# Low parts on VectorE beside the scans, diagonal blocks copied by VectorE, and the FFN norm's steps inside the out-projection

## The chip, the core and the metric

The kernel runs on one core of one Trainium2 chip. The metric is the device time of one execution in microseconds; lower is better. Before the change three runs took 1754.33 to 1760.6 us, with a median of 1757.2 us.

## The reference

One encoder block over 1024 tokens of width 1024, in float32, with these parts in a row:

```python
h = rms_norm(x, norm_mix)
proj = h @ w_in
attn = windowed_gqa(q, k, v, sink)               # q, k, v from proj
rw = rwkv7_time_mix(...)                         # two scans over the tokens, forward and backward
gates = sigmoid(proj[..., O_GATE:].reshape(b, s, 2, D_MODEL))
merged = gates[..., 0, :] * (attn @ w_up_attn) + gates[..., 1, :] * (rw @ w_up_rwkv)
x = x + merged @ w_out
hf = rms_norm(x, norm_ffn)
x = x + square(relu(hf @ w_ff1)) @ w_ff2
hp = rms_norm(x, norm_ple)
x = x + (p @ w_ple) * sigmoid(hp @ w_ple_gate)
```

The change touches the scans, the work that is done beside them, both up-projections, the out-projection and the norm ahead of ff1.

## The kernel before

**Products.** A large product is made of three matmuls over a high and a low part of each operand. `split` makes the parts: ScalarE casts the source to the high part (L189), and another engine subtracts the high part from the source to give the low part (L190). That engine is VectorE if nothing is named; `load_w`, which loads a block of weights and splits it, names GpSimd if nothing is named. TensorE adds the three products hi x hi, hi x lo and lo x hi in PSUM; in the profile they have the lines L230 to L232 (`mm3`) or L212 to L222 (`mmo`, `mm3_steps`). Products that are issued through `mmo` keep the order in which the program names them. The other instructions are ordered by a scheduler, engine by engine, by the program's order and by when their buffers come free. Each engine then works through its own queue in order: an instruction that waits holds up all behind it.

**Scans.** The tokens are cut into 16 chunks of 64. A step `s` of the loop has, for both directions, `products(s + 2)` (masked by VectorE into `gm`, L1115), `u_part` (its result is copied to `UV`, half by VectorE at L1174, half by ScalarE), `s_part` (the state, on VectorE), `y_part`, `wa_part` and `wb_part` (copied to `Wt`, half by VectorE at L1165, half by ScalarE), and `operands`, which transposes on TensorE and lets ScalarE copy the result to `tm` (L1138). Between these parts stand eight gaps. In a gap `fill` takes matmuls from the generator `beside`: first the second branch's gates (`gates(1, ...)`, weights `wst`, `whi`, `wlo`), then the attention's up-projection (`uaps`, weights `wust`, `wuhi`, `wulo`).

**Inverses.** Every four chunks need 32 inverses of 64x64 blocks. `begin_low` and `low` make the lower parts of the next four chunks, one per call, in gaps chosen by `aside`. `inverse` then inverts the 32x32 diagonal blocks by 31 pairs of VectorE operations (L808, L811), `inverse_turned` transposes the result twice on VectorE (`Zn`, `Zt`, L818 and L819), and `inverse_off` makes the block off the diagonal: 64 small products at once (128 matmuls of 32x32, `qps`), copies by ScalarE to `Q`, again 64 products, copies by ScalarE to `zi`. The four diagonal blocks are copied from `Zn` and `Zt` to `zi` by ScalarE too (L839).

**Up-projection of the scans' output (`up_rwkv`, L1348).** 16 groups of 12 matmuls (`mmc`): block m of the weights for the token half e = 1, and `LEAD` = 2 blocks later for e = 0. Each group loads `g1t` and `mgt`, multiplies the one by the product, adds the other (L1360, L1361) and splits the sum to `mh`, `ml` (`mTh[e]`, `mTl[e]`). Beside it the weights of the out-projection are loaded and split (`wo0h`, `wo0l`; later `wo1h`, `wo1l`), the low parts by GpSimd.

**Out-projection and FFN norm.** `out_proj(i, n)` makes 24 matmuls (`mmo`) for token tile i and column half n and adds the result to `x1`. The loop over n = 0 goes first; in the loop over n = 1 a tile of `x1` is complete after its product. The norm of a tile has a step s (`nf_stats`: square on ScalarE, the power on GpSimd), a step c (`nf_scale`: VectorE, 128x1024, L1467, `xs`) and, for the first four tiles, a step t (`nf_tr`: eight transposes `tp` on TensorE, a split to `Fh`, `Fl` and a copy to `raw`). `NFS` says behind which tile of the loop each step is issued. For the last four tiles `second_set(j)` follows the whole loop: eight transposes, differences of them (`t1`, `t2`) on VectorE, and splits to the operands `T2`, `T1`, `B22` of a Strassen-like product. `Fh`, `Fl` are new tiles of the pool that `mh0`, `ml0` used. ff1 (`ff1ps`) then starts with the operands that the first tiles made.

Of the kernel before, what the change touches and what calls it, by code (L numbers as in the profile page):

```python
# [9 lines left out]
F32 = mybir.dt.float32  # L10
# [23 lines left out]
X1AT = 5  # L34
WOAT = (0, 4)

NFS = {2: "s0", 3: "c0 s1", 4: "t0 c1 t1 s2 c2", 5: "t2 s3 c3", 6: "t3 s4 c4", 7: "s5 c5"}
EXPIN = (1, 0)
EPS_AT = (3, 3, 2, 2)
VH = 8  # L40
# [20 lines left out]

FILLEP = 11

LEAD = 2
FILLQ = 8

LOW_AT = 3
# [69 lines left out]
def block_kernel(ctx: ExitStack, tc: tile.TileContext, I: dict, out: bass.AP):  # L137
# [676 lines left out]
    def inverse_turned(pl, Z, behind=None):  # L814

        Zn = pl.tile([P, 32, 32], F32, name="Zn", tag="inv", bufs=3)
        Zt = pl.tile([P, 32, 32], F32, name="Zt", tag="inv", bufs=3)
        a = nc.vector.transpose(out=Zn.rearrange("r p c -> r c p"), in_=Z.rearrange("p r c -> p c r"))  # L818
        b = nc.vector.transpose(out=Zt.rearrange("c p r -> c r p"), in_=Z)  # L819
        if behind:  # L820
            after(a, behind)
            after(b, a)
        return Zn, Zt

    def inverse_off(pl, ps_of, lt, zz, zi, mm, between):

        Zn, Zt = zz
        g = [slice(32 * k, 32 * k + 32) for k in range(4)]
        Q = pl.tile([P, 32, 32], F32, name="Q", tag="inv", bufs=3)
        qss = [ps_of([P, 16, 32], "qps") for _ in range(2)]  # L830
        for i in range(32):
            for r in (0, 2):
                mm(qss[i // 16][g[r + 1], i % 16, :], lt[g[r], i, 32:64], Zn[g[r], i, :], start=True, stop=True)
        for hp, qs in enumerate(qss):
            for r in (1, 3):
                nc.scalar.copy(Q[g[r], 16 * hp:16 * hp + 16, :], qs[g[r]])
        for r0, src_ in ((0, Zt), (32, Zt), (64, Zn), (96, Zn)):
            k = r0 // 32 % 2
            nc.scalar.copy(zi[r0:r0 + 32, :, 32 * k:32 * k + 32], src_[r0:r0 + 32])  # L839
        between()  # L840
        qss = [ps_of([P, 16, 32], "qps") for _ in range(2)]
        for i in range(32):
            mm(qss[i // 16][g[0], i % 16, :], Q[g[1], i, :], Zt[g[1], i, :], start=True, stop=True)
            mm(qss[i // 16][g[3], i % 16, :], Zt[g[3], i, :], Q[g[3], i, :], start=True, stop=True)
        for hp, qs in enumerate(qss):
            nc.scalar.copy(zi[g[0], 16 * hp:16 * hp + 16, 32:64], qs[g[0]])
            nc.scalar.copy(zi[g[3], 16 * hp:16 * hp + 16, 0:32], qs[g[3]])
# [120 lines left out]
    epi = {}  # L968
    wua = I["w_up_attn"].rearrange("(a k p) n -> a p k n", a=2, p=64)
    def beside():  # L970
        yield from gates(1, range(GATT, 2 * KT), mmo)
        sW.close()
        sH1.close()
        epi["RWA"] = pool(sR, "rwA", side="right")
# [1 line left out]
        for h in range(2):  # L976
            hs = slice(512 * h, 512 * h + 512)
            aTh = UA.tile([P, NP, 512], F32R, name="aTh", tag="aTh", bufs=1)
            aTl = UA.tile([P, NP, 512], F32R, name="aTl", tag="aTl", bufs=1)
            for k in range(NP):  # L980
                at = UA.tile([P, 512], F32, name="atl", tag="mgt", bufs=2)
                nc.sync.dma_start(at, at_d[:, k, hs])
                split(aTh[:, k, :], aTl[:, k, :], at)
            def weights(m):
                st = UA.tile([P, NP, P], F32, name="wust", tag="wu_st", bufs=2)
                for a in range(2):
                    nc.sync.dma_start(st[a * 64:a * 64 + 64], wua[a][:, :, m * P:(m + 1) * P])
                hi = UA.tile([P, NP, P], F32R, name="wuhi", tag="wu_hi", bufs=3)
                lo = UA.tile([P, NP, P], F32R, name="wulo", tag="wu_lo", bufs=3)
                split(hi, lo, st, nc.gpsimd)  # L990
                return hi, lo

            ahead = [weights(0), weights(1)]
            if h == 0:
                for _ in range(BRIDGE):
                    yield 1
            for m in range(KT):
                hi, lo = ahead.pop(0)
                if 0 < m < KT - 1:
                    ahead.append(weights(m + 1))  # L1000
                g = UA.tile([P, 512], F32, name="gta", tag="g1t", bufs=2)
                nc.sync.dma_start(g, g_d[m, :, hs])
                ps = PMM.tile([P, 512], F32, name="uaps", tag="mm", bufs=2)
                yield from mm3_steps(ps, [(hi[:, k, :], lo[:, k, :], aTh[:, k, :], aTl[:, k, :]) for k in range(NP)], mmo)
                nc.vector.scalar_tensor_tensor(out=g, in0=g, scalar=1.0, in1=ps, op0=ALU.add, op1=ALU.mult)
                nc.sync.dma_start(mg_d[m, :, hs], g)
                yield
# [243 lines left out]
    for s in range(NCH):  # L1251
# [8 lines left out]
        def aside(i):  # L1260

            b = s // NB + 1
            if b < NCH // NB and (s % NB, i) in ((0, 1), (0, 2), (0, 3), (1, 0)):
                low(b)
                if i == 0:
                    zzs[b] = inverse(BI, lts[b])
            if ep is not None:
                next(ep, None)
# [58 lines left out]
    WO1 = pool(sO, "wo1")  # L1327
    sWS = ExitStack()
    WOS = pool(sWS, "wos")

    def wo_tiles(pl, n):
        wo[n] = [pl.tile([P, KT, 512], F32R, name=f"wo{n}{x_}", bufs=1) for x_ in "hl"]

    def load_wo(n, ks, spl, tag, sbufs):

        for k in ks:
            st = spl.tile([P, 2, 512], F32, name="wst", tag=tag, bufs=sbufs)
            nc.sync.dma_start(st, wov[:, k:k + 2, 512 * n:512 * n + 512])
            split(wo[n][0][:, k:k + 2], wo[n][1][:, k:k + 2], st, nc.gpsimd)

    wo_tiles(WO1, 0)

# [5 lines left out]
    def up_rwkv(m, e):  # L1348

        hi, lo = wu[m]  # L1350
        g = UA.tile([P, 2, 256], F32, name="g1t", tag="g1t", bufs=2)
        nc.sync.dma_start(g, tset(g_d[KT + m], e))
        mg = UA.tile([P, 2, 256], F32, name="mgt", tag="mgt", bufs=2)
        nc.sync.dma_start(mg, tset(mg_d[m], e))
        if (m + e) % 2:
            ps = PF.tile([P, 2, 256], F32, name="mmc", tag="ff1", bufs=3)
# [7 lines left out]
    for m in range(KT + LEAD):  # L1364
# [1 line left out]
            if m == WOAT[n]:  # L1366
                load_wo(0, (4 * n, 4 * n + 2), WOS, "wo_st", 3)
        if m < KT:
            wu[m] = load_w(UA, "wu", wur[:, :, m * P:(m + 1) * P], P, bufs=3, sbufs=2)
            up_rwkv(m, 1)  # L1370
        if m >= LEAD:
            up_rwkv(m - LEAD, 0)
# [8 lines left out]

    sX1, sN, sX0 = (ExitStack() for _ in range(3))
    x1 = [None] * NT
    PX1 = pool(sX1, "x1b", side="right")
    for i in range(4, NT):
        x1[torder[i]] = PX1.tile([P, DM], F32, name=f"x1_{torder[i]}")
    NR = pool(sN, "nrm", bufs=2, side="right")
    PX0 = pool(sX0, "x1a", side="right")
    for i in range(4):
        x1[torder[i]] = PX0.tile([P, DM], F32, name=f"x1_{torder[i]}")  # L1390
    PT = pool(sPF, "psT", space=PSUM, side="right")
    sW1 = ExitStack()
    w1v = I["w_ff1"].rearrange("(k p) n -> p k n", p=P)
    NPR = FF // P // 2
# [35 lines left out]
    with ExitStack() as s7:  # L1430
# [22 lines left out]
        w1_load(0)  # L1453

        raw = [NR.tile([P, 4, 512], F32, name=f"raw{k}", bufs=1) for k in range(2)]
        Fh = AC[0].tile([P, KT, 512], F32R, name="fh", tag="ab0", bufs=1)
        Fl = AC[0].tile([P, KT, 512], F32R, name="fl", tag="ab1", bufs=1)
        right = {"B11": (Fh[:, 0:4], Fl[:, 0:4]), "B21": (Fh[:, 4:8], Fl[:, 4:8])}
        nfs = {}

# [18 lines left out]
                split(Fh[:, 4 * q:4 * q + 4, tsl], Fl[:, 4 * q:4 * q + 4, tsl], tp)  # L1479
                nc.scalar.copy(raw[q][:, :, tsl], tp)  # L1480

        nf = {"s": nf_stats, "c": nf_scale, "t": nf_tr}

        def norm_steps(i):
            for step in NFS.get(i, "").split():
# [2 lines left out]
        for i in range(NT):  # L1488
# [5 lines left out]
                w1_load(1)  # L1494
            t = torder[i]
            nc.sync.dma_start(x1_d[t * P:(t + 1) * P, :], x1[t])
    sX0.close()
    sFO = ExitStack()
    FO = pool(sFO, "fops")
    ACt = [AC[1].tile([P, KT, 512], F32R, name=n, tag=g, bufs=1) for n, g in (("rh", "ab0"), ("rl", "ab1"))]  # L1500
    right["T2"] = tuple(a_[:, 0:4] for a_ in ACt)
    right["B22"] = tuple(a_[:, 4:8] for a_ in ACt)
    for r in ("T1", "T3", "T4"):
        right[r] = tuple(FO.tile([P, 4, 512], F32R, name=r + n) for n in "hl")

    def second_set(j):

        tsl = slice(j * P, (j + 1) * P)
        (_, b12), (_, b22) = nf_quads(4 + j)
        t1, t2 = quad("t1"), quad("t2")  # L1510
        nc.vector.tensor_tensor(out=t1, in0=b12, in1=raw[0][:, :, tsl], op=ALU.subtract)
        nc.vector.tensor_tensor(out=t2, in0=b22, in1=t1, op=ALU.subtract)
        for r, s_ in (("T2", t2), ("T1", t1), ("B22", b22)):
            split(right[r][0][:, :, tsl], right[r][1][:, :, tsl], s_)

        nc.vector.tensor_tensor(out=raw[0][:, :, tsl], in0=t2, in1=raw[0][:, :, tsl], op=ALU.subtract)
        nc.vector.tensor_tensor(out=raw[1][:, :, tsl], in0=raw[1][:, :, tsl], in1=t2, op=ALU.subtract)

    for j in range(4):
        second_set(j)  # L1520
        if j < 2:
            nf_stats(6 + j)
            nf_scale(6 + j)


    sPF.close()
# [43 lines left out]
    for p in range(2):  # L1570
# [3 lines left out]
        product(pb, p, "A12")  # L1574
        first[p] = pb
        if p == 0:
            w1_op(1, "A11")
            w1_op(1, "A12")
    for r, q in (("T3", 0), ("T4", 1)):
        for k in (0, 2):  # L1580
            split(right[r][0][:, k:k + 2], right[r][1][:, k:k + 2], raw[q][:, k:k + 2])
    sN.close()
    sX1.close()
    sFP = ExitStack()
# [323 lines left out]
```

## Time and profile before

| | us |
|---|---|
| median of three runs | 1757.2 |
| the profiled execution | 1762.18 |
| its span | 1760.4 |
| PE busy | 1679.0 |
| DVE busy | 1129.6 |
| ACT busy | 895.6 |
| POOL busy | 209.7 |

The profile comes from one execution. PE is TensorE, DVE is VectorE, ACT is ScalarE, POOL is GpSimd and SP is the engine that issues most transfers; PEld is the load of weights into TensorE, which overlaps PE. PEclk is the clock that was granted to TensorE, as a share of the full one. In a row of the timeline stand the start, the duration, the engine, the line, the operation, the tiles and in brackets the idle time ahead of it with what ended it. Durations of neighbours overlap: on PE and DVE an instruction starts before the one ahead has ended, so the step from start to start counts.

### The profile page before, as it was taken

The numbers are of one execution on the slowest core, as the hardware profiler recorded it, in microseconds if no ns is written. First come the engines' busy times: TensorE is split into PE (matmuls) and PEld (weight loads), VectorE is DVE, ScalarE is ACT, GpSimd is POOL, SyncE is SP. The second block draws the span as 40 slices with busy tenths as digits, with TensorE's granted clock in tenths as the row PEclk, the third lists the DMA queues.
The fourth block names the chain that finished last, engine by engine and source line by source line (L and its number), as shares of the span: only waits on it lengthen the run. The fifth ranks groups of instructions, "written<-read, shape, count | busy, mean of one in ns | idle before, by whom it ended". The sixth has DMA issues, their size and how long they took to land. (4 is left out here: it accounts for less than half of the span.)

```text
span 1760.4 us, 29968 instructions
## 1 busy us (share of the span) xinstructions
PE 1679.0 (95%) x11544; PEld 1352.9 (77%) x11544; DVE 1129.6 (64%) x1977; ACT 895.6 (51%) x1636; POOL 209.7 (12%) x210
## 2 busy tenths in 40 slices
PE   7999999899999989898799989999999999999998
PEld 6987777666677777676578867888888888888887
DVE  5658998176829393855661587776776877685432
ACT  5548886287664646564521455444444444554221
POOL 3430000421312122121412000000000000000000
PEclk9999999999999999999999989999999999999999
DMA  6353666846364544455753215445448974574111
GB/s 214 80 147 102 176 187 174 243 121 163 102 180 122 144 127 122 133 149 178 220 181 113 108 61 191 138 151 168 138 154 286 306 238 127 167 227 142 56 39 40
DMA packets 274239, 269.20 MB, mean 153 GB/s; under 512 B 47920, under 2 KB 196272, under 8 KB 274096
## 3 DMA queue, kind: packets, MB, share of 16 engines
q1 hardware_dynamic: 264160, 254.18, 46.5%
q0 software_dynamic: 9792, 12.59, 2.8%
q8 instruction: 91, 1.49, 0.4%
q10 hardware_dynamic: 144, 0.52, 0.1%
q14 instruction: 52, 0.43, 0.1%
HBM read 186.49 MB, written 80.74 MB: 152 GB/s over the span
## 5 line engine op out<-in xcount | busy, mean ns | idle before, releaser
L1790 PE MATMUL ff2ps<-th,sl 128*128 128x512 f32 x448 | 174.5, 390 | 0.0
L1790 PE MATMUL ff2ps<-tl,sh 128*128 128x512 f32 x448 | 174.5, 390 | 0.0
L1790 PE MATMUL ff2ps<-th,sh 128*128 128x512 f32 x448 | 174.1, 390 | 0.0
L189 ACT CAST sh<-sst 128x512 fp32r<-128x512 f32 x109 | 67.8, 622 | 106.0 <-PE ff2ps L1790 55.9
L190 POOL TENSOR_TENSOR wlo<-wst,whi 128x512 fp32r<-128x512 f32 x66 | 85.9, 1311 | 280.3 <-ACT whi L189 231.0
L174 POOL TENSOR_TENSOR rstd<-ms,neghalf 128x1 f32<-128x1 f32 x24 | 13.2, 553 | 793.5 <-DVE ms L172 793.5
L190 DVE TENSOR_TENSOR sl<-sst,sh 128x512 fp32r<-128x512 f32 x109 | 75.1, 689 | 48.5 <-ACT sh L189 48.0
L1790 PEld LDWEIGHTS ff2ps<-th,sh 128*128 128x128 f32 x448 | 84.1, 188 | 17.9 <-ACT th L189 0.3
L1790 PEld LDWEIGHTS ff2ps<-tl,sh 128*128 128x128 f32 x448 | 84.1, 188 | 17.5
L1790 PEld LDWEIGHTS ff2ps<-th,sl 128*128 128x128 f32 x448 | 84.1, 188 | 17.3
L189 ACT CAST whi<-wst 128x512 fp32r<-128x512 f32 x100 | 59.9, 617 | 65.2 <-DMA wst<-in_w_in_dram 32.5
L189 ACT CAST w1h<-w1st 128x512 fp32r<-128x512 f32 x48 | 28.4, 620 | 103.8 <-DMA w1st<-in_w_ff_dram 64.0
L190 DVE TENSOR_TENSOR w1l<-w1st,w1h 128x512 fp32r<-128x512 f32 x48 | 31.8, 687 | 50.5 <-ACT w1h L189 50.5
L218 PE MATMUL gmm<-hh,whi 128*128 128x512 f32 x136 | 55.6, 409 | 2.5 <-ACT whi L189 2.5
L1115 DVE TENSOR_TENSOR gm<-gps,gmask 128x512 f32<-128x512 f32 x64 | 42.1, 683 | 23.6 <-PE gps L212 23.6
L222 PE MATMUL gmm<-hh,wlo 128*128 128x512 f32 x136 | 55.7, 410 | 0.0
L220 PE MATMUL gmm<-hl,whi 128*128 128x512 f32 x136 | 55.5, 408 | 0.0
L808 DVE TENSOR_TENSOR tmp<-Lp,Z 128x31 f32<-128x31 f32 (+15 forms) x124 | 51.3, 414 | 4.6 <-POOL Z L803 1.8
L190 DVE TENSOR_TENSOR w1l<-ssum,w1h 128x512 fp32r<-128x512 f32 x64 | 43.0, 687 | 16.1 <-ACT w1h L189 16.1
L1540 PE MATMUL ff1ps<-rh,w1h 128*128 128x512 f32 x128 | 50.1, 391 | 1.7 <-ACT w1h L189 1.7
L1540 PE MATMUL ff1ps<-fh,w1l 128*128 128x512 f32 x128 | 51.1, 399 | 0.6 <-DVE w1l L190 0.6
L212 PE MATMUL gmm<-hh,wlo 128*128 128x512 f32 x120 | 51.4, 429 | 0.0
(410 smaller groups left out, 4927.4 us busy)
## 6 DMA issues: line engine op xcount, KB each, us to landing
wst<-in_w_in_dram SPq DMA_DIRECT2D x92, 256.0 KB, 3.3
tst<-in_w_ff_dram SPq DMA_DIRECT2D x80, 256.0 KB, 3.8
w1st<-in_w_ff_dram SPq DMA_DIRECT2D x32, 512.0 KB, 5.1
hid_S<-h SPq DMA_DIRECT2D x64, 256.0 KB, 2.1
sst<-hid_S SPq DMA_DIRECT2D x64, 256.0 KB, 2.7
hid_A<-h SPq DMA_DIRECT2D x48, 256.0 KB, 2.1
sst<-hid_A SPq DMA_DIRECT2D x45, 256.0 KB, 3.7
ra_d<-ra SPq DMA_DIRECT2D x8, 1024.0 KB, 5.9
```

The source lines that it names most:

```text
L174: nc.gpsimd.tensor_tensor(out=r, in0=ms, in1=neghalf.broadcast_to([P, width]), op=ALU.pow)
L189: a = nc.scalar.copy(hi, src)
L190: b = (lo_eng or nc.vector).tensor_tensor(out=lo, in0=src, in1=hi.bitcast(F32), op=ALU.subtract)
L212: tc.keep_in_program_order(nc.tensor.matmul(*a, **kw))
L218: mm(ps, ah, bh, start=(i == 0), stop=False)
L220: mm(ps, ah, bl, start=False, stop=False)
L222: mm(ps, al, bh, start=False, stop=(i == n - 1))
L808: nc.vector.tensor_tensor(out=tv, in0=Lp[:, t + 1:32, t:t + 1].broadcast_to([P, n, m]), in1=Z[:, t:t + 1, 0:m].broadcast_to([P, n, m]), op ...
L1115: nc.vector.tensor_tensor(out=gm[d][:, s % NB, q::2, :], in0=pss[q], in1=gmask[:, d, :].unsqueeze(1).broadcast_to([P, NP, P]), op=ALU.mult)
L1540: nc.tensor.matmul(ps, x_[:, k, :], y_[:, k, :], start=start and k + i == 0, stop=k == 3 and i == 2, skip_group_check=True)
L1790: nc.tensor.matmul(banks[bs][i], x_[:, isl], y_, start=fresh and p + j == 0, stop=p == NPR - 1 and j == 2, skip_group_check=True)
```

## The change

It has five parts.

1. The norm's steps are issued inside the n = 1 loop, a tile behind its product: `NFS` now has s, c, then t of the tile before, and a new step p, which is `second_set(0..2)` behind tiles 5 to 7; `second_set(3)` follows ff1's first product. `Fh`, `Fl` are `mTh[0]`, `mTl[0]` themselves, written in place; `T2` and `B22` are `mTh[1]`, `mTl[1]`; `T1` takes the buffers of the first four `x1` tiles, which now lie in two pairs. The transposes' PSUM has a pool of its own.
2. The four diagonal blocks of an inverse are copied by VectorE, ordered behind the second transpose.
3. The low parts of gates(1), of `w_up_attn`, of `w_up_rwkv` and of `w_out` are made by VectorE instead of GpSimd.
4. `aside` takes the four `low` calls in the gaps of the first step of four instead of three there and one in the second step, and `inverse` follows at that step's end.
5. `LEAD` is 1 instead of 2, and `g1t`, `mgt` of `up_rwkv` have a pool of their own.

```diff
-NFS = {2: "s0", 3: "c0 s1", 4: "t0 c1 t1 s2 c2", 5: "t2 s3 c3", 6: "t3 s4 c4", 7: "s5 c5"}
+NFS = {0: "s0 c0", 1: "s1 c1 t0", 2: "s2 c2 t1", ..., 5: "s5 c5 p0", 6: "s6 c6 p1", 7: "s7 c7 p2"}
-LEAD = 2
+LEAD = 1
...
-        return Zn, Zt
+        return Zn, Zt, b if behind else None
...
-            nc.scalar.copy(zi[r0:r0 + 32, :, 32 * k:32 * k + 32], src_[r0:r0 + 32])
+            a = nc.vector.tensor_copy(zi[r0:r0 + 32, :, 32 * k:32 * k + 32], src_[r0:r0 + 32])
+            if behind:
+                after(a, behind)
...
-        yield from gates(1, range(GATT, 2 * KT), mmo)
+        yield from gates(1, range(GATT, 2 * KT), mmo, lo_of=lambda m: nc.vector)
-                split(hi, lo, st, nc.gpsimd)
+                split(hi, lo, st)
...
-            if b < NCH // NB and (s % NB, i) in ((0, 1), (0, 2), (0, 3), (1, 0)):
+            if b < NCH // NB and (s % NB, i) in ((0, 0), (0, 1), (0, 2), (0, 3)):
                 low(b)
-                if i == 0:
+                if i == 3:
                     zzs[b] = inverse(BI, lts[b])
...
+    GP = pool(sWS, "gup")
-            split(wo[n][0][:, k:k + 2], wo[n][1][:, k:k + 2], st, nc.gpsimd)
+            split(wo[n][0][:, k:k + 2], wo[n][1][:, k:k + 2], st)
-        g = UA.tile([P, 2, 256], F32, name="g1t", tag="g1t", bufs=2)
+        g = GP.tile([P, 2, 256], F32, name="g1t", bufs=2)
-        mg = UA.tile([P, 2, 256], F32, name="mgt", tag="mgt", bufs=2)
+        mg = GP.tile([P, 2, 256], F32, name="mgt", bufs=2)
-            wu[m] = load_w(UA, "wu", wur[:, :, m * P:(m + 1) * P], P, bufs=3, sbufs=2)
+            wu[m] = load_w(UA, "wu", wur[:, :, m * P:(m + 1) * P], P, bufs=3, sbufs=2, lo_eng=nc.vector)
...
-        Fh = AC[0].tile([P, KT, 512], F32R, name="fh", tag="ab0", bufs=1)
-        Fl = AC[0].tile([P, KT, 512], F32R, name="fl", tag="ab1", bufs=1)
+        Fh, Fl = mTh[0], mTl[0]
...
+        right["T2"] = tuple(a_[:, 0:4] for a_ in (mTh[1], mTl[1]))
+        right["B22"] = tuple(a_[:, 4:8] for a_ in (mTh[1], mTl[1]))
+        def second_set(j):
+            if j == 0:
+                right["T1"] = tuple(PX0.tile([P, 4, 512], F32R, name="T1" + n, tag=f"x1a{i}", bufs=1) for i, n in enumerate("hl"))
...
-    for j in range(4):
-        second_set(j)
-        if j < 2:
-            nf_stats(6 + j)
-            nf_scale(6 + j)
...
         if p == 0:
+            second_set(3)
             w1_op(1, "A11")
             w1_op(1, "A12")
```

How this moves instructions is seen at three places. The first is ACT's queue at the end of the inverse that step 7 of the scans waits for; L839 are the diagonal blocks, L1138 the copies `tm`, L836 those to `Q`. Before:

```order
526 L1190 COPY Sb_4608<-Tc 64x8x64
527 L1210 COPY y<-yps 128x4x64 x2
528 L839 COPY zi<-Zn 32x32x32 x2
529 L839 COPY zi<-Zt 32x32x32
530 L1138 COPY tm<-tmps 128x512 x2
531 L316 ACTIVATE gth<-gmm 128x512
532 L836 COPY Q<-qps 32x512 x4
533 L839 COPY zi<-Zt 32x32x32
```

And after, where `tm` has the line L1140:

```order
524 L1192 COPY Sb_4608<-Tc 64x8x64
525 L1212 COPY y<-yps 128x4x64 x2
526 L1140 COPY tm<-tmps 128x512 x2
527 L189 CAST whi<-wst 128x512
528 L316 ACTIVATE gth<-gmm 128x512
529 L836 COPY Q<-qps 32x512 x4
```

The four copies are gone from the queue, and `tm` stands directly behind `y`. The second is DVE's queue at the end of the same inverse, with `Wt` (L1165, after: L1167) as the next thing that the scan needs. Before:

```order
824 L1191 COPY Sb_4608<-Tc 64x8x64
825 L1194 TENSOR_TENSOR Sc<-Tc,Dt 128x512
826 L818 STREAM_TRANSPOSE Zn<-Z 128x32x32
827 L819 STREAM_TRANSPOSE Zt<-Z 128x32x32
828 L1165 COPY Wt<-wps 64x512
829 L1115 TENSOR_TENSOR gm_4605<-gps,gmask 128x4x128 x2
830 L1174 COPY UV<-ups 64x512
```

After:

```order
844 L1193 COPY Sb_4608<-Tc 64x8x64
845 L1196 TENSOR_TENSOR Sc<-Tc,Dt 128x512
846 L818 STREAM_TRANSPOSE Zn<-Z 128x32x32
847 L819 STREAM_TRANSPOSE Zt<-Z 128x32x32
848 L839 COPY zi<-Zn 32x32x32
849 L839 COPY zi<-Zt 32x32x32 x2
850 L839 COPY zi<-Zn 32x32x32
851 L190 TENSOR_TENSOR wlo<-wst,whi 128x512 x2
852 L1167 COPY Wt<-wps 64x512
853 L1117 TENSOR_TENSOR gm_4605<-gps,gmask 128x4x128 x2
854 L1176 COPY UV<-ups 64x512
```

Between `Zt` and `Wt` there are now the four diagonal blocks and two low parts of gate weights. The third is PE's queue where the out-projection (`mmo`) ends and ff1 begins; `tp` are the norm's transposes, four for half a tile. Before:

```order
4092 L232 MATMUL mmo<-wo1h,ml_9463 128x512
4093 L1473 MATMUL tp<-ident,xs 128x128 x8
4094 L1540 MATMUL ff1ps<-fh,w1h 128x512
4095 L1540 MATMUL ff1ps<-fl,w1h 128x512
4096 L1540 MATMUL ff1ps<-fh,w1l 128x512
4097 L1473 MATMUL tp<-ident,xs 128x128 x4
...
4123 L1540 MATMUL ff1ps<-fh,w1h 128x512
4124 L1540 MATMUL ff1ps<-fl,w1h 128x512
4125 L1473 MATMUL tp<-ident,xs 128x128 x12
```

After:

```order
4094 L232 MATMUL mmo<-wo1h,ml_9466 128x512
4095 L1479 MATMUL tp<-ident,xs 128x128 x8
4096 L1541 MATMUL ff1ps<-mh_9463,w1h 128x512
4097 L1541 MATMUL ff1ps<-ml_9464,w1h 128x512
...
4119 L1541 MATMUL ff1ps<-mh_9463,w1l 128x512
4120 L1479 MATMUL tp<-ident,xs 128x128 x8
4121 L1541 MATMUL ff1ps<-mh_9463,w1h 128x512
```

Before, 32 transposes are left when the last `mmo` is issued, and twelve of them stand in one row; after, 16 are left, and between the two groups of eight lie 24 matmuls of ff1.

More of the change, by code (lines that the diff above doesn't have):

```diff
@@ L35 @@
 WOAT = (0, 4)
-NFS = {2: "s0", 3: "c0 s1", 4: "t0 c1 t1 s2 c2", 5: "t2 s3 c3", 6: "t3 s4 c4", 7: "s5 c5"}
+NFS = {0: "s0 c0", 1: "s1 c1 t0", 2: "s2 c2 t1", 3: "s3 c3 t2", 4: "s4 c4 t3", 5: "s5 c5 p0", 6: "s6 c6 p1", 7: "s7 c7 p2"}
 EXPIN = (1, 0)
@@ L822, in inverse_turned @@
             after(b, a)
-        return Zn, Zt
+        return Zn, Zt, b if behind else None
     def inverse_off(pl, ps_of, lt, zz, zi, mm, between):
-        Zn, Zt = zz
+        Zn, Zt, behind = zz
         g = [slice(32 * k, 32 * k + 32) for k in range(4)]
@@ L1383, in block_kernel @@
     x1 = [None] * NT
+    PX0 = pool(sX0, "x1a", side="right")
+    for j in range(2):
+        pair = PX0.tile([P, 2, DM], F32, name=f"x1a{j}", tag=f"x1a{j}", bufs=1)
+        for i in range(2):
+            x1[torder[2 * j + i]] = pair[:, i]
     PX1 = pool(sX1, "x1b", side="right")
@@ L1387, in block_kernel @@
     NR = pool(sN, "nrm", bufs=2, side="right")
[L1388 to L1391, printed above, removed]
+    sPT = ExitStack()
+    PT = pool(sPT, "psT", space=PSUM, side="right")
     sW1 = ExitStack()
@@ L1480, in nf_tr @@
                 nc.scalar.copy(raw[q][:, :, tsl], tp)
-        nf = {"s": nf_stats, "c": nf_scale, "t": nf_tr}
+        right["T2"] = tuple(a_[:, 0:4] for a_ in (mTh[1], mTl[1]))
[3 more added lines that the diff above has]
+                right["T1"] = tuple(PX0.tile([P, 4, 512], F32R, name="T1" + n, tag=f"x1a{i}", bufs=1) for i, n in enumerate("hl"))
+            tsl = slice(j * P, (j + 1) * P)
+            (_, b12), (_, b22) = nf_quads(4 + j)
+            t1, t2 = quad("t1"), quad("t2")
+            nc.vector.tensor_tensor(out=t1, in0=b12, in1=raw[0][:, :, tsl], op=ALU.subtract)
+            nc.vector.tensor_tensor(out=t2, in0=b22, in1=t1, op=ALU.subtract)
+            for r, s_ in (("T2", t2), ("T1", t1), ("B22", b22)):
+                split(right[r][0][:, :, tsl], right[r][1][:, :, tsl], s_)
+            nc.vector.tensor_tensor(out=raw[0][:, :, tsl], in0=t2, in1=raw[0][:, :, tsl], op=ALU.subtract)
+            nc.vector.tensor_tensor(out=raw[1][:, :, tsl], in0=raw[1][:, :, tsl], in1=t2, op=ALU.subtract)
+        nf = {"s": nf_stats, "c": nf_scale, "t": nf_tr, "p": second_set}
         def norm_steps(i):
@@ L1496, in block_kernel @@
             nc.sync.dma_start(x1_d[t * P:(t + 1) * P, :], x1[t])
-    sX0.close()
     sFO = ExitStack()
     FO = pool(sFO, "fops")
[L1500 to L1503, printed above, removed]
+    for r in ("T3", "T4"):
         right[r] = tuple(FO.tile([P, 4, 512], F32R, name=r + n) for n in "hl")
[L1506 to L1517, printed above, removed]
-    for j in range(4):
-        second_set(j)
-        if j < 2:
-            nf_stats(6 + j)
-            nf_scale(6 + j)
     sPF.close()
@@ L1581, in block_kernel @@
             split(right[r][0][:, k:k + 2], right[r][1][:, k:k + 2], raw[q][:, k:k + 2])
+    sPT.close()
     sN.close()
@@ L1794, in block_kernel @@
                 sFP.close()
+                sX0.close()
                 PXX = pool(sX, "x1", side="right")
```

## The prediction

> **What bounds the kernel now.** I read the page's busy shares first, then PE's waits, then windows with the granted clock, then the timelines around the longest waits.
>
> ```profile
> span 1760.4 us, 29968 instructions
> PE 1679.0 (95%) x11544; PEld 1352.9 (77%) x11544; DVE 1129.6 (64%) x1977; ACT 895.6 (51%) x1636; POOL 209.7 (12%) x210
> ```
>
> TensorE works 1679.0 of 1760.4 us. The diff takes no matmul away, so it can win only two things: the 81 us in which PE stands still, and the time in which PE runs at half clock. The waits that the change touches, columns us in total, times, longest:
>
> ```profile
> PE qps L212 <- ACT tm L1138: 6.5, 3, 3.3
> PE sps L212 <- DVE UV L1174: 5.9, 6, 1.8
> PE mmc L232 <- POOL wlo L190: 5.3, 5, 2.8
> PE ups L212 <- DVE Wt L1165: 4.7, 5, 1.6
> PE tp L1473 <- DVE rl L190: 3.4, 2, 1.9
> PE tp L1473 <- DVE xs L1467: 2.0, 1, 2.0
> PE mmc L230 <- ACT whi L189: 1.9, 1, 1.9
> ```
>
> They fall into three places: the scans (about 480 to 815 us), up_rwkv (858 to 917) and the FFN norm (1010 to 1033). The windows of these places, columns: PE, PEld, DVE, ACT, POOL busy, then PEclk:
>
> ```profile
> 520.00:560.00 40.00, 36.26 (x524) 29.57 (x523) 32.41 (x70) 19.67 (x41) 7.65 (x9) 0.96 0.54 151
> 560.00:600.00 40.00, 37.51 (x767) 30.55 (x766) 19.60 (x31) 25.16 (x51) 10.54 (x11) 0.96 0.33 96
> 640.00:680.00 40.00, 36.39 (x645) 29.20 (x645) 23.18 (x42) 23.99 (x47) 6.45 (x7) 0.96 0.30 92
> 720.00:760.00 40.00, 34.40 (x617) 28.66 (x611) 29.81 (x62) 25.11 (x47) 7.24 (x8) 0.83 0.59 162
> 880.00:920.00 40.00, 37.52 (x146) 28.80 (x147) 24.49 (x35) 9.20 (x15) 5.11 (x4) 0.93 0.56 172
> 1000.00:1040.00 40.00, 33.91 (x153) 26.82 (x152) 33.80 (x51) 19.50 (x34) 2.20 (x4) 0.87 0.10 40
> ```
>
> Each of these windows holds a dip of the clock. What a dip costs is read from PE's timeline at the end of the norm (start, duration, operation):
>
> ```profile
> 1021.00 0.63 PE L1473 MATMUL tp<-ident,xs 128*128 128x128 f32 x4 [1.51 <-DVE rl L190]
> 1023.67 1.09 PE L1473 MATMUL tp<-ident,xs 128*128 128x128 f32 x4 [2.05 <-DVE xs L1467]
> 1028.98 0.63 PE L1540 MATMUL ff1ps<-fh,w1h 128*128 128x512 f32 x1
> 1031.96 0.63 PE L1540 MATMUL ff1ps<-fl,w1h 128*128 128x512 f32 x1
> ...
> 1035.05 0.39 PE L1540 MATMUL ff1ps<-fh,w1l 128*128 128x512 f32 x1
> 1040.26 0.39 PE L1540 MATMUL ff1ps<-T1h,w1l 128*128 128x512 f32 x1
> 1042.17 0.50 PE L1540 MATMUL ff1ps<-rh,w1h 128*128 128x512 f32 x1 [1.52 <-ACT w1h L189]
> ```
>
> From 1028.98 to 1031.96 lie 7 steps of 0.426 us, from 1035.05 to 1040.26 lie 23 of 0.2265. So a microsecond at half clock loses 1 - 0.2265/0.426 = 0.47 us, and a window whose clock is c has been at half for 2(1 - c) of PE's busy time.
>
> **The change part by part. Norm.** The transposes and second_set leave the stretch behind out_proj, where DVE is the bound, and go between the tiles of the n = 1 loop. That loop starts here, and its steps and one group of eight transposes are:
>
> ```profile
> 962.13 0.40 PE L230 MATMUL mmo<-wo1h,mh 128*128 128x512 f32 x1
> 963.77 0.40 PE L231 MATMUL mmo<-wo1l,mh 128*128 128x512 f32 x1
> ...
> 1010.59 1.04 PE L1473 MATMUL tp<-ident,xs 128*128 128x128 f32 x8
> 1011.38 0.47 PE L1540 MATMUL ff1ps<-fh,w1h 128*128 128x512 f32 x1
> ```
>
> A step is 1.64/7 = 0.2343 us and eight transposes hold PE 0.79 us. Ahead of the product that starts at 1042.17 the same work stands in both orders: 8 x 24 matmuls of out_proj (45.0 us), 8 groups of transposes (6.3) and 72 of ff1 (16.3), 67.6 us in all. Without a wait it ends at 962.1 + 67.6 = 1029.7. I add 0.3 for a late first transpose and keep the wait of 1.52 and the 0.4 of drain ahead of it, since that wait is for a buffer that PE itself frees: 1031.9 in place of 1042.2. **Gain 10 us.** DVE has to follow. Its work on a tile with second_set (i = 5 to 7) is one scaling and eight operations of 128x512: the residual add, t1, t2, the low parts of T2, T1 and B22, and two updates of raw. Each starts 0.60 after the one before in a full queue, the scaling takes 1.20 (0.08 less than its row):
>
> ```profile
> 1016.57 1.28 DVE L1467 SCALAR_TENSOR_TENSOR xs<-x,rstd,gainf 128x1024 f32<-128x1024 f32 x1
> 1018.37 0.68 DVE L190 TENSOR_TENSOR T1l<-t,T1h 128x512 fp32r<-128x512 f32 x1
> ```
>
> 1.20 + 8 x 0.60 = 6.0 and some 0.3 for small ones, 6.3 us, against 24 x 0.2343 + 0.79 = 6.4 on PE. It fits with nothing to spare. If it doesn't, each of three tiles loses up to 1.3 us: range 6 to 11. T1 takes the buffers of the first four x1 tiles and so waits for their stores, which leave two tiles, 12.8 us, earlier; a store isn't late by that much. SP issues the same transfers in nearly the same order.
>
> **up_rwkv.** Here PE waits behind GpSimd:
>
> ```profile
> 875.87 2.35 POOL L190 TENSOR_TENSOR wo0l<-wst,wo0h 128x1024 fp32r<-128x1024 f32 x1 [3.55 <-ACT wo0h L189]
> 878.19 1.71 POOL L190 TENSOR_TENSOR wlo<-wst,whi 128x512 fp32r<-128x512 f32 x1
> ...
> 876.43 2.35 DVE L1361 TENSOR_TENSOR g1t<-g1t,mgt 128x512 f32<-128x512 f32 x1
> 881.08 0.69 DVE L1361 TENSOR_TENSOR g1t<-g1t,mgt 128x512 f32<-128x512 f32 x1
> ```
>
> A weight's low part waits behind a low part of w_out, and the same DVE line takes 2.35 us while GpSimd subtracts and 0.69 when it doesn't. On DVE a low part is 0.6 to 0.7, of w_out 1.28. DVE's load per m is then 7 x 0.7 = 4.9 us against 24 matmuls, 5.6; the four w_out parts add 5.1 once, where they delay what is queued behind them (the g1t products that free PSUM). The waits for POOL (5.3) and for whi (1.9, a buffer that LEAD = 1 frees a group sooner) go, and with them the dip: 2 x 0.07 x 37.5 x 0.47 = 2.5. Of these 9.7 I take **8**; 3 if the loads of g1t and mgt, now in two buffers of their own, become the pace; at most 10.
>
> **Scans.** At each of three inverse ends ACT copies diagonal blocks before the tm copies on which PE waits:
>
> ```profile
> 572.57 2.10 ACT L839 COPY zi<-Zn 32x1024 f32<-32x1024 f32 x2 [1.55 <-DVE Zn L818]
> 575.65 1.05 ACT L1138 COPY tm<-tmps 128x512 f32<-128x512 f32 x2
> 576.27 2.21 PE L212 MATMUL qps<-Zn,lt 32*32 32x32 f32 x128 [1.61 <-ACT tm L1138]
> 585.26 0.68 DVE L1165 COPY Wt<-wps 64x512 f32<-64x512 f32 x1 [10.79 <-PE wps L212]
> ```
>
> DVE is idle there for 10.79 us, so four copies cost no time: no row has one on DVE; ACT's 1.04 and the 1.28 of the 128x1024 scaling above put it near 1, at most 1.3, so four take 5.2. Were the idle time gone, three ends would pay 15.6. The 6.5 us of waits go. The dips of 560:600 and 640:680 (0.08 of the busy time at half) lose 1.4 each, that of 720:760 (0.34 x 34.4 us) 5.5: 8.3 in all. That is 14.8 gross. Against it: 46 subtracts of gates(1) and up_attn move to DVE's queue, 46 x 0.69 = 32 us, and 12 copies, together some 45 us in the 320 us of the scans. The four windows of scans above have DVE at 105 of 160 us, 66%; 45 in 320 make it 80%. Each subtract waits for ACT's cast, and behind it stand Wt and UV, for which PE waits 10.6 us already. They win something too: GpSimd slows DVE in the inverse,
>
> ```profile
> 543.36 2.88 POOL L190 TENSOR_TENSOR wlo<-wst,whi 128x512 fp32r<-128x512 f32 x2 [10.33 <-ACT whi L189]
> 543.71 1.37 DVE L811 TENSOR_TENSOR Z<-Z,tmp 128x247 f32<-128x247 f32 x1
> 545.12 1.39 DVE L808 TENSOR_TENSOR tmp<-Lp,Z 128x252 f32<-128x252 f32 x1
> 546.55 0.42 DVE L811 TENSOR_TENSOR Z<-Z,tmp 128x252 f32<-128x252 f32 x1
> ```
>
> 1 us per subtract of its own stall for 0.69 of work now. But steps with no inverse have only the load. I put one more subtract's wait on two thirds of 16 UV copies, 16 x 0.69 x 0.6 = 7. **Net gain 8**; range 15 (no new wait) to -6 (the same wait before Wt and UV, and the dips half kept). Low products in one step's four gaps, and the inverse at that step's end, cost nothing as long as PE has gate matmuls to fill with; otherwise they lie in that range, as do ACT's four Lc copies, which come to stand ahead of its half of Wt. GpSimd's queue loses its subtracts, so the memsets behind them (UV, Z) come no later. The attention's first inverse moves four copies too: within 1 us.
>
> The profiled execution took 1762.2 us, 1.8 of it around the span and 5.0 above the median of 1757.2. 1762.2 - 10 - 8 - 8 = **1736 us**; from the median it would be 1731, and I keep the 5 for waits that I didn't find.
>
> **The rivals.** *VectorE's queue beside the scans becomes the bound (slower).* Two subtracts, which wait for a cast, stand ahead of both Wt and UV in every step: 32 x 2 x 0.69 = 44 us in place of my 7. Then 1762 - 33 + 44 = 1773. For it: 520:560 has DVE at 32.41 of 40 now. Against: the idle 10.79 at Wt. It decides once PE's waits for UV and Wt pass 10.6 + 33 = 44 us. [...] Chance 0.12.
>
> *The clock dips stay at the inverse ends.* The 128 products of 32x32 last 2.21 us with little work, directly behind the wait; if they bring the clock down, only 6.5 of the 14.8 is won, which the 7 of new waits eats: 1744. [...] The window 560:600 shows 0.96 behind a wait of 1.61 alone, so I hold the wait for the cause. Chance 0.17.
>
> *Norm and up_rwkv give half.* DVE's tile takes 7.5 us in place of 6.3 and loads pace up_rwkv: gains 6 and 3, 1745 with the scans' 8; the change then doesn't do what its order says. Chance 0.16.
>
> *GpSimd's interference was dearer than I count.* No new wait (+7) and half of the 10.6 for UV and Wt gone (+5): 1724. Chance 0.15.
>
> **How the numbers follow.** My forecast of 1736 has 0.40. All three terms at their ends at once would give 1726 and 1759. I give 1722 to 1757: it holds the third and second rival and the fourth at 1724, and leaves out the slower one (0.12) and some 0.05 at the ends. A measurement here can tell 0.3% from no change, 5 us: faster is below 1752. Rivals two to four lie there, with spread above it, the first lies above: faster 0.79, same 0.09, slower 0.12.
>
> **What would show it.** Right: PE's waits for tm, for POOL's wlo and for rl at the norm transposes are gone, the windows 560:600, 720:760, 880:920 have a clock of 0.98 or more, the product at 1042 starts 26 us sooner. Wrong: waits for UV and Wt above 20 us in total, a dip behind the first qps without a wait ahead of it, transposes that wait for xs, mmc that waits for DMA.

## The result, and the profile after

The changed kernel takes 1731.26 us (median of 4 runs, 1726.71 to 1734.54) against 1757.39 us before (4 runs): a ratio of 0.9845, 95% interval 0.981 to 0.9881. It is 26 us faster. The forecast was 1736, the range 1722 to 1757. The profiled execution took 1726.7 us and is the fastest of its four, while that of before (1762.2) is slower than all four of before, so the two profiles lie 35.5 us apart, 9 more than the medians. One execution of the run with the block copies alone, at 2383.58 us and a granted clock of 0.64, ran in a slower state and is left out of its median.

The page's first lines after:

```profile
span 1724.9 us, 29927 instructions
PE 1666.1 (97%) x11544; PEld 1344.1 (78%) x11544; DVE 1165.3 (68%) x2055; ACT 879.8 (51%) x1620; POOL 123.0 (7%) x148
```

PE's busy time fell by 12.9 us with the same number of matmuls. The mean granted clock rose from 0.980 to 0.991, so by estimate most of that is time at half clock. PE's idle time fell from 81.4 to 58.8 us, 22.6 less. The two make the 35.5. Of PE's waits after, those on the changed path:

```profile
PE pt L935 <- DVE smk L932: 4.8, 6, 3.1
PE uaps L212 <- ACT aTh L189: 4.0, 2, 3.3
PE mmc L230 <- DVE g1t L1363: 2.1, 3, 0.9
PE ups L212 <- DVE Wt L1167: 1.8, 1, 1.8
PE sps L212 <- DVE UV L1176: 1.5, 2, 0.8
PE uaps L212 <- DVE wulo L190: 1.3, 1, 1.3
PE mmo L230 <- ACT mh L189: 1.1, 1, 1.1
PE tp L1479 <- DVE xs L1473: 0.5, 1, 0.5
```

The waits for tm (6.5) and for GpSimd's wlo (5.3) are gone. Those for UV and Wt, which I had expected to grow, fell from 10.6 to 3.3. New are the waits for g1t and mh at the up-projection, and the waits for smk, ahead of the scans, grew from 2.6 to 4.8. The windows that were shown of before (PE, PEld, DVE, ACT, POOL busy, then PEclk):

```profile
520.00:560.00 40.00, 38.45 (x546) 31.11 (x544) 36.45 (x88) 21.12 (x45) 2.33 (x4) 1.00 0.52 145
560.00:600.00 40.00, 39.91 (x851) 32.54 (x848) 21.28 (x30) 24.66 (x53) 3.21 (x6) 1.00 0.50 139
640.00:680.00 40.00, 40.00 (x844) 32.97 (x843) 22.22 (x32) 24.38 (x50) 3.20 (x6) 1.00 0.55 153
720.00:760.00 40.00, 37.25 (x673) 30.39 (x670) 31.13 (x47) 27.68 (x52) 2.25 (x4) 0.91 0.64 186
880.00:920.00 40.00, 38.02 (x165) 30.41 (x165) 20.76 (x28) 8.27 (x11) 0.00 (x0) 1.00 0.59 191
1000.00:1040.00 40.00, 38.08 (x165) 30.50 (x164) 31.61 (x50) 19.12 (x35) 0.00 (x0) 1.00 0.48 157
```

The clock is full in all but 720 to 760. DVE works more beside the scans, up to 36.45 of 40 us, and PE waits less. The norm's end, where the transposes stand among ff1's matmuls:

```profile
991.90 0.63 PE L1479 MATMUL tp<-ident,xs 128*128 128x128 f32 x4 [0.30 <-DVE ml L190]
1005.35 0.50 PE L1541 MATMUL ff1ps<-mh,w1h 128*128 128x512 f32 x1 [1.51 <-ACT w1h L189]
```

The last row is the product that started at 1042.17 before, so it comes 36.8 us sooner.

To compare stages I take the first and last starts of PE's groups in each profile, and the time between them: to the first `wps` (attention and all before it), to the last `ups` (scans), to the first `mmc` (second epilogue), to the first `mmo` of the n = 1 loop (up_rwkv and the n = 0 loop), to the first `ff2ps` (norm and ff1), to the last `plps`.

| us | start | scans | epilogue | up, n = 0 | norm, ff1 | rest | run |
|---|---|---|---|---|---|---|---|
| before | 490.4 | 320.5 | 47.4 | 103.8 | 369.9 | 422.9 | 1762.2 |
| after | 490.8 | 302.5 | 47.5 | 92.8 | 363.0 | 422.9 | 1726.7 |
| difference | +0.4 | -18.0 | +0.1 | -11.0 | -6.9 | 0.0 | -35.5 |

My terms were -8 for the scans, -8 for up_rwkv, -10 for the norm. These are single profiles, and the one of before is slow. Profiles of the experiments below that leave a stage as it was have 317.3 and 316.4 us for the scans, 101.7 to 103.0 for up_rwkv with the n = 0 loop, and 369.4 to 370.4 for the norm with ff1. Against these the changed kernel gains 14 to 15 us in the scans, 9 to 10 in up_rwkv and 6 to 7 in the norm.

### The profile page after: what moved, and what is told of

It reads as the page before. It is cut to its first block, busy times and chain, and to the rows that moved or that the text cites. A ratio compares the mean times of both kernels' runs of the same rounds, so it can differ in the third digit from the quotient of the medians.

```text
span 1724.9 us, 29927 instructions
## 1 busy us (share of the span) xinstructions
PE 1666.1 (97%) x11544; PEld 1344.1 (78%) x11544; DVE 1165.3 (68%) x2055; ACT 879.8 (51%) x1620; POOL 123.0 (7%) x148
## 4 chain that ended last, share of the span: by engine, by line
PE 73%; DVE 13%; DMA 6%; ACT 5%; issue 3%; POOL 1%; SPq 0%; DVEq 0%; ACTq 0%; POOLq 0%
PE ff2ps L1793 18%; PE ff1ps L1541 16%; PE gmm L212 3%; DMA wst<-in_w_in_dram 2%; DVE tmp L808 2%; DVE Z L811 2%; PE plps L222 2%; PE plps L218 2%; PE plps L220 2%; PE mm L230 2%; PE mm L232 2%; PE mm L231 2%; PE uaps L212 1%; PE po L943 1%; PE gps L212 1%
## 5 line engine op out<-in xcount | busy, mean ns | idle before, releaser
L1541 PE MATMUL ff1ps<-mh,w1h 128*128 128x512 f32 x256 | 100.3, 392 | 1.9 <-ACT w1h L189 1.9
L1541 PE MATMUL ff1ps<-ml,w1h 128*128 128x512 f32 x256 | 99.9, 390 | 0.0
L1541 PE MATMUL ff1ps<-mh,w1l 128*128 128x512 f32 x256 | 99.6, 390 | 0.0
L174 POOL TENSOR_TENSOR rstd<-ms,neghalf 128x1 f32<-128x1 f32 x24 | 14.8, 616 | 924.2 <-DVE ms L172 924.2
L190 DVE TENSOR_TENSOR wlo<-wst,whi 128x512 fp32r<-128x512 f32 x72 | 48.5, 687 | 22.7 <-ACT whi L189 22.4
L1541 PEld LDWEIGHTS ff1ps<-mh,w1h 128*128 128x128 f32 x256 | 48.1, 188 | 12.9 <-ACT w1h L189 2.8
L1541 PEld LDWEIGHTS ff1ps<-mh,w1l 128*128 128x128 f32 x256 | 48.1, 188 | 10.8 <-DVE w1l L190 0.6
L222 PE MATMUL gmm<-hh,wlo 128*128 128x512 f32 x136 | 55.5, 408 | 0.5 <-POOL wlo L190 0.5
L1541 PEld LDWEIGHTS ff1ps<-ml,w1h 128*128 128x128 f32 x256 | 48.1, 188 | 10.0
```

The source lines that it names most:

```text
L190: b = (lo_eng or nc.vector).tensor_tensor(out=lo, in0=src, in1=hi.bitcast(F32), op=ALU.subtract)
L222: mm(ps, al, bh, start=False, stop=(i == n - 1))
L1541: nc.tensor.matmul(ps, x_[:, k, :], y_[:, k, :], start=start and k + i == 0, stop=k == 3 and i == 2, skip_group_check=True)
```

## The experiments

All times stand beside runs of the kernel before on the same chip (medians 1759.85 in the first group of four, 1759.87 in the second, 1761.27 and 1761.53 in the rest).

**One part each.** The block copies alone:

```diff
-            nc.scalar.copy(zi[r0:r0 + 32, :, 32 * k:32 * k + 32], src_[r0:r0 + 32])
+            a = nc.vector.tensor_copy(zi[r0:r0 + 32, :, 32 * k:32 * k + 32], src_[r0:r0 + 32])
```

> The kernel before with one part of the change: the four diagonal blocks of an inverse are copied by VectorE. Theory (the tm copies were late because ScalarE's queue held the block copies, and the clock fell behind these waits): the 6.5 us of PE's waits for tm go, and the dips at the second and third of them too; 10 to 15 us faster. Rival (the 32x32 products bring the clock down by themselves): only the waits go, 6 us faster, and the windows behind the first 32x32 products still show a clock of 0.8 or less.

Measured: 1756.85 us (median of 11), ratio 0.9982 (0.9969 to 0.9995), 3 us faster, where 10 to 15 were expected. The scans did what was expected in kind: 310.0 in place of 320.5, the wait for tm 0.2 us in all. But the start grew from 490.4 to 495.6. Its profile shows why, first GpSimd, then VectorE, then PE, at the inverse that is made beside the attention:

```profile
472.56 2.55 POOL L190 TENSOR_TENSOR wlo<-wst,whi 128x512 fp32r<-128x512 f32 x2 [5.78 <-ACT whi L189]
475.04 1.85 POOL L1102 MEMSET Sb<- 128x1024 f32 x2
476.83 0.96 POOL L1102 MEMSET Wt<- 128x1024 f32 x1
477.73 1.53 POOL L1130 MEMSET UV<- 64x512 f32 x2
479.34 3.25 POOL L190 TENSOR_TENSOR wlo<-wst,whi 128x512 fp32r<-128x512 f32 x2
```

```profile
474.12 4.68 DVE L839 COPY zi<-Zn 32x1024 f32<-32x1024 f32 x1
478.81 2.66 DVE L839 COPY zi<-Zt 32x1024 f32<-32x1024 f32 x2
481.49 2.12 DVE L839 COPY zi<-Zn 32x1024 f32<-32x1024 f32 x1
```

```profile
484.38 2.04 PE L212 MATMUL gps<-rac,bkc 64*128 64x128 f32 x12 [4.71 <-DVE gm L1117]
```

A block copy on VectorE takes 4.68 us while GpSimd works without a break, and the masks `gm` stand behind it, for which PE waits 4.71. In the changed kernel each of the 16 block copies takes 0.67 to 0.69. Those of a later inverse:

```profile
570.72 0.69 DVE L839 COPY zi<-Zn 32x1024 f32<-32x1024 f32 x1
571.42 1.38 DVE L839 COPY zi<-Zt 32x1024 f32<-32x1024 f32 x2
```

The low parts beside the scans alone (`lo_of=lambda m: nc.vector` for the second branch's gates, `split(hi, lo, st)` for `w_up_attn`):

> The kernel before with one part of the change: the low parts of the second branch's gates and of the attention's up-projection are made by VectorE. Theory (GpSimd's subtracts stretch VectorE's steps of the inverse, and so UV and Wt come late): PE's waits for UV and Wt fall from 10.6 to about 4 us, 4 to 8 us faster. Rival (VectorE's queue is the bound beside the scans): these waits rise above 15 us, and the time is the same or longer by up to 7 us.

Measured: 1754.0 us, ratio 0.9956 (0.9935 to 0.9976), 6 us faster. The theory's wait went: UV doesn't appear any more, Wt once. But its profile has another in its place:

```profile
PE qps L212 <- ACT tm L1138: 6.2, 2, 3.1
PE qps L212 <- DVE Zn L818: 3.8, 1, 3.8
PE ups L212 <- DVE Wt L1165: 1.7, 1, 1.7
```

PE comes sooner to the inverse's end and waits there: 3.1 us for tm where it was 1.6. The scans took 318.6, no less than in profiles that leave them as they were (316.4 to 320.5), so the profile doesn't show where the 6 us lie.

The up-projection's parts alone (low parts of its weights and of `w_out` on VectorE, LEAD 1, the pool for `g1t` and `mgt`):

> The kernel before with the up-projection's parts of the change: low parts of its weights and of the out-projection's on VectorE, LEAD 1, the loads in a pool of their own. Theory: the waits for GpSimd's wlo (5.3 us), for whi (1.9) and the dip (2.5) go: 8 to 12 us faster. Rival (the loads of g1t and mgt set the pace): 3 us faster, with mmc waiting for transfers or for the g1t products behind them.

Measured: 1748.01 us, ratio 0.993 (0.9909 to 0.9951), 12 us faster; up_rwkv and the n = 0 loop took 94.1 in place of 103.8. The theory holds: the waits for wlo and whi are gone. Of the rival's waits there are 2.2 us for g1t, and none of mmc for a transfer.

The norm alone (`NFS`, tiles in place, `second_set` in the loop):

> The kernel before with the FFN norm's part of the change alone. Theory: the transposes and second_set fit beside the out-projection's second loop; from that loop's first matmul to the product that waits for w1h it takes 72 us in place of 80; 7 to 10 us faster. Rival (VectorE is full there): PE waits for xs or the low parts between the tiles, and 4 us or less are won.

Measured: 1754.7 us, ratio 0.9965 (0.9951 to 0.998), 6 us faster, a little less than expected; norm and ff1 took 363.4 in place of 369.9, as in the changed kernel.

The low products' place alone:

```diff
-            if b < NCH // NB and (s % NB, i) in ((0, 1), (0, 2), (0, 3), (1, 0)):
+            if b < NCH // NB and (s % NB, i) in ((0, 0), (0, 1), (0, 2), (0, 3)):
```

> The kernel before with one part of the change: the four low products in one step's gaps, and the inverse at that step's end. Theory: nothing waits for an inverse before its four steps are over, so within 2 us of before. Rival (ScalarE's copies Lc ahead of Wt, or VectorE's inverse between the scans' steps): 2 to 5 us slower, with the waits for Wt above 7 us.

Measured: 1757.98 us, ratio 0.9986 (0.9969 to 1.0003): no difference that can be told.

**Do the parts need each other?** Block copies and low parts beside the scans together:

> The kernel before with two parts at once: the diagonal blocks copied by VectorE and the low parts of the gates and of the attention's up-projection made by VectorE. Theory (the parts need each other: a block copy took 4.68 us in the run of the first part alone while GpSimd was at work, 0.69 otherwise): more than the two alone, 3.2 + 7.7 = 10.9 us; 14 to 18 us faster, and the first block copies take 0.7 us. Rival (the parts only add up): 9 to 12 us faster.

Measured: 1740.74 us, ratio 0.9892 (0.987 to 0.9915), 19 us faster, where the two alone make 3.0 + 5.9 = 9 by their medians and 0.62% = 11 by their ratios. The parts do more than add up. The scans took 299.6 us, 21 less than before, the start 491.1. Each part removes what spoiled the other: without GpSimd's work the copies take 0.7, and without ScalarE's copies PE doesn't wait for tm.

**Is VectorE's queue the bound?** The changed kernel, with each low part beside the scans subtracted twice:

```diff
+            nc.vector.tensor_tensor(**kw)
             return nc.vector.tensor_tensor(**kw)
```

> The changed kernel with every low part of the gates and of the attention's up-projection subtracted twice on VectorE, so that it has 46 x 0.69 = 32 us more work beside the scans. Theory (VectorE is idle where it counts): up to 5 us slower than the changed kernel, so 21 us or more faster than before. Rival (VectorE's queue is nearly the bound): most of the 32 us shows, the waits for UV and Wt pass 15 us, and the kernel is about as slow as before.

Measured: 1732.95 us, ratio 0.9846 (0.9822 to 0.9869), the same as the changed kernel's 0.9845. 32 us more work cost nothing that can be told. The first rival falls.

**What does GpSimd's work beside VectorE cost?** The changed kernel, with a useless subtract on GpSimd for each of 30 on VectorE (it changes no result):

```diff
             a = nc.vector.tensor_tensor(**kw)
+            nc.gpsimd.tensor_tensor(out=junk, in0=kw["in1"], in1=kw["in1"], op=kw["op"])
             return a
```

> The changed kernel, in which GpSimd makes a useless subtract of 128x512 for each of VectorE's 30 of the gates, that nothing waits for. Theory (GpSimd's subtracts hold up VectorE's operations beside them): steps of the inverse of 1.3 us come back, PE's waits for UV and Wt rise from 3.3 to 7 us or more, block copies take over 1 us; 4 to 8 us slower than the changed kernel. Rival (it was the wait for GpSimd's result that cost time): within 2 us of the changed kernel.

Measured: 1738.29 us, ratio 0.9881 (0.9857 to 0.9905), 5 us above the run with doubled subtracts beside it. The two intervals overlap a little, but no single run of the one reaches the other's (1735.22 to 1742.32 against 1730.63 to 1733.84), and the profile shows what GpSimd's work did. GpSimd, VectorE and PE's waits:

```profile
544.86 2.22 POOL L193 TENSOR_TENSOR junk<-whi 128x512 f32<-128x512 f32 x2 [10.58 <-ACT whi L200]
```

```profile
544.29 0.42 DVE L819 TENSOR_TENSOR tmp<-Lp,Z 128x256 f32<-128x256 f32 x1
...
545.22 0.95 DVE L822 TENSOR_TENSOR Z<-Z,tmp 128x256 f32<-128x256 f32 x1
546.21 1.15 DVE L819 TENSOR_TENSOR tmp<-Lp,Z 128x255 f32<-128x255 f32 x1
```

```profile
PE sps L223 <- DVE UV L1187: 4.0, 2, 2.0
PE ups L223 <- DVE Wt L1178: 3.1, 4, 1.8
```

Nothing waits for the useless results, PE doesn't wait for whi, which they read, anywhere beside the scans, and yet the inverse's steps take 1 us in place of 0.42, PE waits 7.1 us for UV and Wt in place of 3.3, and the scans take 309.9. Block copies mostly stayed at 0.7, one reached 1.4; that part of the expectation missed.

**Where does the sum of the parts go?** Pair, up-projection, norm and low products' place make 19.0 + 12.3 + 6.2 + 2.4 = 40 us, the whole made 26.

> The changed kernel once more, for a second profile and beside the two that follow. The parts tried alone and in one pair add up to 40 us (19.0 + 12.3 + 6.2 + 2.4), the changed kernel won 26. Theory (the first profile of it, 1726.7, was its fastest run): 1731 to 1733 us, and the stages show where the 10 us between it and the sum lie. Rival (the sum is right): 1725 us or less.

Measured: 1732.8 us, ratio 0.9835 (0.9809 to 0.9862), 29 us faster. The theory holds, and 11 to 14 us are missing. The second profile of the changed kernel has the start at 494.8, the scans at 303.2, the others within 0.5 of the first. The start differs by as much between the four profiles that have neither the block copies nor the low parts on VectorE: 490.4 before, 488.2, 491.6 and 487.2 with the up-projection, the norm and the low products' place alone. In the eight that have both it is 490.1 to 494.9, by their means 3 us longer (the last section shows a wait there). So the stages of single profiles don't tell where the missing time lies. It was looked for in two parts.

> The changed kernel without the part that draws the low products into one step. In the run of the block copies and low parts together the scans took 299.6 us, with that part too 302.5. Theory (that part costs where VectorE has more to do): 2 to 5 us faster than the changed kernel. Rival (it does nothing, as alone): within 2 us.

Measured: 1727.68 us, ratio 0.9805 (0.9777 to 0.9834), 5 us below the changed kernel beside it; the scans took 300.3 in place of 303.2. In the same two profiles the start is 4.6 us shorter and up_rwkv with the n = 0 loop 3.8 longer, so they don't show that the 5 us are all this part's.

> The changed kernel with LEAD 2 again. Theory (LEAD 1 frees a weight's buffer a group sooner): the wait for whi comes back, 2 to 3 us, less the 1 us wait for mh at the out-projection's start: 1 to 2 us slower than the changed kernel. Rival (the subtracts on VectorE alone did it): the same or up to 2 us faster.

Measured: 1729.55 us, ratio 0.9812 (0.9786 to 0.9839), 3 us below it, where I expected it above. In its profile the waits for g1t are 0.4 us and that for mh is gone; in the changed kernel they are 2.1 and 1.1. The wait for whi that LEAD 1 was to remove is 0.2.

> The changed kernel without the part that draws the low products into one step and with LEAD 2. Taken singly against the changed kernel beside them (1732.8) the two gave 1727.7 and 1729.6. Theory (they act in different stages): 1724 to 1725 us, a ratio of 0.979. Rival (the two differences are scatter between runs): 1730 to 1733 us, 0.983.

Measured: 1727.03 us, ratio 0.9805 (0.9779 to 0.9831). The two don't add up; it is no better than without the low products' place alone. Both lie below the changed kernel's 1732.8, by 0.3%, with intervals that still overlap. These two are the fastest versions measured. Without the low products' place the parts add up to 37.5 us, and that kernel won 34 (29 to 39 by its interval): what is then missing lies within the noise.

## Why the prediction was right, and where it was not

The direction, the sum and the three places were right. That the sum came so close is in part luck: I took too little for the scans, too much for the norm, and nothing for the start, which came to be longer. Point by point:

- *From which time.* I took 25.6 us off the profiled 1762.2 and kept its 5 us above the median "for waits that I didn't find". From the median the same terms gave 1731, which is what came. The profiled run's surplus was scatter.
- *Scans, -8.* The gross gain of 14.8 was right in kind: the waits for tm went. **The step that failed is the 7 us of new waits on UV.** No new wait came: UV and Wt fell to 3.3, and doubled subtracts cost nothing. The scans' gain was 18 in the two profiles, 14 to 15 against profiles with the scans as they were. This is the fourth rival's mechanism (no new wait, more than half of the 10.6 gone), to which I gave 0.15; the useless subtracts and the pair of parts show it.
- *A block copy at 0 to 1.3 us* held with GpSimd quiet (0.67 to 0.69) and not beside its subtract and memsets (4.68). I priced part 2 without looking at what GpSimd does there; alone it would have been worth 3 us, since the first inverse, put down as "within 1 us", cost some 5.
- *The dips belong to the waits, but not to them alone.* The second rival, by which the dips would have stayed, fell: 560 to 600 has 1.00 with the same 32x32 products. Still the products had a share in these dips, and a wait of 1.6 us brought one in the profile before and none with the low products' place alone (last section), so 8.3 for three dips was a price for one execution, not for all. Of the signs that I named, 720 to 760 missed: its clock is 0.91 and not 0.98, so by the sum that gave 5.5 us for its dip some 3.2 are still lost there.
- *up_rwkv, -8.* 11.0 in the profiles together with the n = 0 loop, 12 by time alone. The waits and the dip that I priced at 9.7 went; LEAD 1, priced as a help for whi, brought waits for g1t and mh of 3.2; with LEAD 2 they are 0.4.
- *Norm, -10.* Mis-sized: from the first matmul of the n = 1 loop (933.6) to the product at 1005.35 it took 71.7 us in place of 69.8, with 0.5 for xs and 0.3 for a low part among it, and 1.4 of the gain was lost again before ff2. 6.9 remain. The third rival's 6 was nearer.
- *GpSimd's memsets "come no later".* They came sooner, and that had a price that I didn't see: those of Sb started at 477.30 before, behind two subtracts, and at 465.78 after, where they hold up the attention's scaling of smk (last section).
- *The low products' place, "costs nothing".* Alone nothing that can be told; in the changed kernel probably about 5 us (0.9835 against 0.9805, with intervals that overlap). That it is VectorE's inverse between more of its own work was argued from the windows (36.45 of 40 us busy in 520 to 560), not shown.

## What to carry to other kernels

Before moving a copy to VectorE look at what GpSimd does in that window, and before leaving a subtract on GpSimd look at what VectorE does: the two parts were worth 3 and 6 us apart and 19 together. Spare time of an engine that isn't waited for told more here than its busy share: VectorE, busy for 36 of 40 us in places, took another 32 us for nothing. Try a bundle's parts singly in the full bundle too; one of five seems to have cost time there that it did not cost alone.

## What the runs showed of the hardware

A copy and a scaling on VectorE were held over a whole row of GpSimd instructions, not just over one: the block copy above took 4.68 us over a subtract and a row of memsets (0.67 to 0.69 in the changed kernel), and in the changed kernel, before the scans, a scaling took 3.21 us where the next of its kind took 0.34:

```profile
464.58 1.26 POOL L190 TENSOR_TENSOR wlo<-wst,whi 128x512 fp32r<-128x512 f32 x1 [1.57 <-ACT whi L189]
465.78 1.84 POOL L1102 MEMSET Sb<- 128x1024 f32 x2
```

```profile
464.56 3.21 DVE L932 TENSOR_SCALAR smk<-smk,es 128x256 f32<-128x256 f32 x1
467.69 0.28 DVE L811 TENSOR_TENSOR Z<-Z,tmp 128x135 f32<-128x135 f32 x1
467.89 0.34 DVE L932 TENSOR_SCALAR smk<-smk,es 128x256 f32<-128x256 f32 x1
```

That is the wait of 3.1 us for smk, of which the longest was 0.7 in the profile before. In the nine profiles with the gates' low parts on VectorE it is 2.2 or 3.1, in the five without 0.7 or 1.3. GpSimd's next instructions ran before VectorE's one had ended: the two memsets from 465.78 to 467.62 us, within the scaling's 464.56 to 467.77. Whether VectorE stood still all that time, and by what the one engine holds up the other, the rows don't show.

The clock. Behind the same wait of 1.6 us for tm it fell in one execution and not in another. The traces show where the two differ. In all 14 the granted clock is full or half, and it changes only on a grid of 3.413 us. The profile before has 12 whole stretches at half clock of 3.413 to 13.653 us, 1 to 4 times 3.413, and between them stretches at full clock of 13.653 to 727.04 us, 4 to 213 times. The profile after has 6 whole stretches at half, 1 to 3 times 3.413, and between them 3 to 262 times at full. Windows cut on that grid, of the kernel before (its wait ends at 576.27, the prediction shows the row):

```profile
571.86:575.27 3.41, 2.80 (x17) 1.00 0.80 228
575.27:578.68 3.41, 2.41 (x129) 1.00 0.40 149
578.68:582.10 3.42, 3.42 (x16) 0.50 0.03 10
```

And of the one with the low products' place alone:

```profile
571.13 2.21 PE L212 MATMUL qps<-Zn,lt 32*32 32x32 f32 x128 [1.63 <-ACT tm L1138]
```

```profile
568.15:571.56 3.41, 1.78 (x33) 1.00 0.60 193
571.56:574.98 3.42, 3.42 (x121) 1.00 0.23 81
574.98:578.39 3.41, 3.41 (x146) 1.00 0.02 5
```

In the first, the step ahead of the dip holds 1.0 us of the wait and the 2.1 us of 32x32 products behind it. In the second, one step holds the whole wait and the next one most of the products, and the clock stays full. I counted the steps at full clock from 100 to 1715 us of all 14 traces by the time in which PE stood idle in them. Idle for 2 us or more: half clock followed in 67 of 67. Under 0.8 us: in none of 6157, though 57 of these hold 1.8 us or more of 32x32 products. From 0.8 to 1.45 us: in 8 of 130, and each of the 8 holds 1.0 to 2.3 us of such products. From 1.45 to 2 us: in 34 of 91. The profiles before and after alone have, in the same order, 8 of 8, 0 of 874, 1 of 20 and 8 of 14. So in these traces products of 32x32 alone brought no dip, and the 8 dips behind 0.8 to 1.45 us of idle time all had such products in the same step. Whether the wait of 1.6 us cost a dip went, in the two executions above, with where the grid fell; that this is a part of the kernel's scatter of some 5 us is an estimate of mine and was not tested.
